# A fourth unit of seven products in the first down-projection, and sums of weights made ahead and kept in DRAM

## The chip, the cores and the metric

The kernel runs on one core of a Trainium2 chip. Its time is the device time of one execution in microseconds, and times of several executions are told as a median with the lowest and the highest. A profile of one further execution shows every instruction of the five engines: TensorE (PE, matrix products; PEld, the loading of its stationary operand), VectorE (DVE), ScalarE (ACT), GpSimd (POOL) and SyncE (SP, which issues nearly all transfers here).

## The reference, cut to what matters

Two transformer layers on 256 tokens of width 1024 in float32. Each layer has an attention and then a gated feed-forward block with a causal convolution of width 3:

```python
def conv_ffn(h, w_up, conv_w, conv_b, w_down):
    S_ = h.shape[1]
    u = h @ w_up
    up = jnp.pad(u, ((0, 0), (CONV_W - 1, 0), (0, 0)))
    u = conv_b + sum(conv_w[j] * up[:, j:j + S_] for j in range(CONV_W))
    gate, val = jnp.split(u, 2, axis=-1)
    return (jax.nn.silu(gate) * val) @ w_down

for l in range(DEPTH):
    ...
    x = x + o.transpose(0, 2, 1, 3).reshape(B_, S_, N_HEADS * HEAD_DIM) @ w_o
    x = x + conv_ffn(rmsnorm(x, ffn_norm[l]), w_up[l], conv_w[l], conv_b[l], w_down[l])
return rmsnorm(x, final_norm)
```

`w_up` is 1024 x 5632 and `w_down` 2816 x 1024 in each layer. The change concerns `w_down` and the loading of the weights.

## The kernel before

**Weights.** All weights come from DRAM in units of 128 x 2048 float32 (1 MB), numbered in the order of use: the attention of layer 0, 22 units of its up-projection (`U_UP0` on), its down-projection (`U_DN0` on), the projections of layer 1's attention, and the same two for layer 1. `fetch` loads a unit into one of three raw buffers ("raw", `wr` in the trace; loads are L184). `prepare` plans the work on it: ScalarE copies it to a rounded high part (`hi_part`, L216, `wh`), VectorE subtracts to get the low part (`lo_part`, L224, `wl`). Each has four buffers. A product is made of three matmuls on `F32R` operands: high activations by high weights, high by low, low by high. `used(i)` says that unit i's matmuls have been written down, and plans the preparation of unit i + 4. When the last low part of a unit is written down, its raw buffer is given to the unit three places on in the order of loads (`NEXT`).

**Up-projection.** Each of the 22 units gives 128 gate and 128 value columns in 48 matmuls (L780 to L782). `post` makes the convolution taps, the gate and high and low parts of the result (L817 to L837), four buffers of 256 columns, one pair of units to a tile.

**Down-projection.** `Down` walks over eleven units (i = 0 to 10); each is two blocks of 128 rows, with 256 tokens as two blocks of 128 and 1024 output columns as two halves of 512. An ordinary unit is eight block products of three matmuls with 512 columns (`mm`, L635 to L638). A unit in `SEVEN` is done in seven block products (`seventh`, L662 to L664), by a scheme that needs four sums of activation blocks (`mix` on GpSimd, `split` L852 and L856 for their high and low parts) and four sums of weight blocks. Those sums form a unit of their own, the "ninth" (`SUMS`): number `slot(layer, i) + 1`, right behind unit i's. It isn't loaded: `sums_of` makes it on VectorE from unit i's raw buffer, in one addition of 1024 columns (L199) and two of 512 (L203), into two buffers of the pool "q". Then it gets high and low parts like any unit (`wh<-sums`, `wl<-sums`). Of unit i itself only three of four column blocks get a high and a low part. Four of the seven products go to PSUM banks of their own (`one`, `six`, `five`, `sev`), three to the ordinary accumulators (`a00`, `a01`, `a10`). After the last unit of seven, `gather` adds the four banks into the residual `xr` (L676 on VectorE and GpSimd, one copy L679 on ScalarE). Layer 0 has seven products in units 3, 5 and 7, layer 1 in 3, 5, 7 and 8. Units 9 and 10 come last, row block by row block, and `add` (L754) adds each accumulator to `xr`; then PE transposes `xr` (L336) for the next projection.

**Order.** TensorE's order is written by hand. The other work is put off with `chain`: steps with due times on a clock that counts TensorE's work, which `tick` runs when they are due and `need` or `require` when a product asks for them. From the first attention on, a planner may shift instructions of the engines around that order.

At the end of layer 1, `tail` (L1206 on) handles the last 512 columns in two halves of 256; it follows a chain of squares, roots and scalings on ScalarE and VectorE.

Of the kernel before, what the change touches and what calls it, by code (L numbers as in the profile page):

```python
# [7 lines left out]
F32 = mybir.dt.float32  # L8
# [3 lines left out]
ALU = mybir.AluOpType  # L12
AX = mybir.AxisListType

P = 128
# [14 lines left out]
UNIT = 2048  # L30
# [20 lines left out]
U_UP0 = 16  # L51
U_DN0 = U_UP0 + NF

SEVEN = ((3, 5, 7), (3, 5, 7, 8))
U_KV = U_DN0 + NF // 2 + len(SEVEN[0])
U_QB = U_KV + 2
U_OB = U_QB + 4
U_UP1 = U_OB + 4
U_DN1 = U_UP1 + NF
N_UNITS = U_DN1 + NF // 2 + len(SEVEN[1])  # L60


def slot(layer, i):
    return (U_DN0, U_DN1)[layer] + i + sum(k < i for k in SEVEN[layer])


SUMS = [slot(l_, i_) + 1 for l_ in range(2) for i_ in SEVEN[l_]]
RAW = {}
for k_ in range(N_UNITS):
    if k_ not in SUMS:  # L70
        RAW[k_] = len(RAW)
NEXT = {k_: min((j_ for j_ in RAW if RAW[j_] == n_ + 3), default=N_UNITS) for k_, n_ in RAW.items()}


@with_exitstack
def trunk(ctx: ExitStack, tc, x, xw, pos, cpk, fin, w, out):
    nc = tc.nc
    one = ctx.enter_context(tc.tile_pool(name="one", bufs=1))
    qd = ctx.enter_context(tc.tile_pool(name="qd", bufs=15))
    wk = ctx.enter_context(tc.tile_pool(name="wk", bufs=2))  # L80
    wp = ctx.enter_context(tc.tile_pool(name="wp", bufs=4))
    ps = ctx.enter_context(tc.tile_pool(name="ps", bufs=2, space=bass.MemoryType.PSUM))

    uid = [0]

# [49 lines left out]
    clock = [0.0]  # L135
    put_off = []
# [8 lines left out]
    def tick(ns):  # L145
        clock[0] += ns
        while put_off and not busy[0]:
            item = min(put_off, key=lambda t: t[0])
            if item[0] > clock[0]:
                return  # L150
            run_item(item)
# [13 lines left out]
    def require(*key):  # L165

        while True:
            mine = [t for t in put_off if t[1] == key]
            if not mine:
                return  # L170
            run_item(min(mine, key=lambda t: t[0]))
# [5 lines left out]
    raws = {}  # L177
    w_time = [0.0]

    def fetch(i):  # L180
        if i < N_UNITS and i not in SUMS:
            raws[i] = wp.tile([P, UNIT], F32, tag="raw", name=f"wr{i}", bufs=3)
            for c in (slice(0, UNIT // 2), slice(UNIT // 2, UNIT)) if 2 <= i < 10 else (slice(0, UNIT),):
                nc.sync.dma_start(raws[i][:, c], w[RAW[i]][:, c])  # L184

    def raw_of(i, c):

        if i not in SUMS:
            return raws[i][:, c]
        t, at = raws[i][c.start // 1024], c.start % 1024  # L190
        return t[:, at:at + c.stop - c.start]
# [38 lines left out]
    def weights(i):  # L230
        wq[i] = (spaced(wp, UNIT, F32R, "hi", f"wh{i}", 4),
                 spaced(wp, UNIT, F32R, "lo", f"wl{i}", 4))

    def prepare(i):

        if i >= N_UNITS:
            return
        n = 4 if i <= 5 or 1 <= i - U_UP0 <= 3 or 1 <= i - U_UP1 <= 3 or U_KV <= i <= U_OB else 2
        cut = [slice(k * UNIT // n, (k + 1) * UNIT // n) for k in range(n)]
        w_time[0] = max(clock[0] + 200.0, w_time[0] + (2500.0 if i - 1 in SUMS else 4500.0), 34000.0 if i == 7 else 0.0)  # L240
        if i == U_KV + 1:
            w_time[0] = max(w_time[0], clock[0] + 3300.0)

        def first():
            if i in SUMS:
                require("t", i)
            weights(i)
            hi_part(i, cut[0])

        def last():  # L250
            lo_part(i, cut[-1])
            if i + 1 in SUMS:
                require("t", i + 1)
            if i not in SUMS:
                fetch(NEXT[i])
            if i + 2 in SUMS:
                sums_of(i + 2)

        if i + 1 in SUMS:
            cut[1] = slice(UNIT // 2, 3 * UNIT // 4)  # L260
        steps = [(w_time[0] - clock[0], first)]
        for k in range(n - 1):
            steps.append((2000.0 / n, lambda k=k: lo_part(i, cut[k])))
            steps.append((2000.0 / n, lambda k=k: hi_part(i, cut[k + 1])))
        chain(("w", i), *steps, (2000.0 / n, last))

    def used(i):

        prepare(i + 4)
# [16 lines left out]
    for c in range(KC):  # L286
        t, at = (first[c // 2], KC * (c == 1) + c % 2 * CH) if c < 6 else (first[c - 3], 0)
# [329 lines left out]
    class Down:  # L617
# [26 lines left out]
        def seventh(self, i):  # L644

            u = self.at(i)
            need(u)
            need(u + 1)
            self.wait(i)
            if not self.more:  # L650
                self.more = [bank(t) for t in ("u", "t", "u", "t")]
            one, five, six, sev = self.more
            (rh, rl), (th, tl) = wq[u], wq[u + 1]
            xh, xl = self.parts[2 * i]
            (a00, a01), (a10, _) = self.acc
            own = dict(start=i == SEVEN[self.layer][0], stop=i == SEVEN[self.layer][-1])
            for o, x_, hi, lo, k, mine in ((one, 0, rh, rl, 0, True), (six, 6, th, tl, 2, True), (five, 5, th, tl, 0, True),
                                           (sev, 4, th, tl, 1, True), (a00, 2, rh, rl, 1, False), (a01, 7, rh, rl, 2, False),
                                           (a10, 3, th, tl, 3, False)):
                o, wh, wl = pairs(o), turns(hi[:, half(k)]), turns(lo[:, half(k)])  # L660
                c = blk(x_)
                nc.tensor.matmul(o, xh[:, c], wh, start=mine and own["start"], stop=False)  # L662
                nc.tensor.matmul(o, xh[:, c], wl, start=False, stop=False)
                nc.tensor.matmul(o, xl[:, c], wh, start=False, stop=mine and own["stop"])  # L664
                tick(3 * 512 / 2.4)
            if own["stop"]:
                self.gather()

# [16 lines left out]
        def units(self, lo, hi):  # L685
            for i in range(lo, hi):
                if self.layer is not None and i in SEVEN[self.layer]:
                    self.seventh(i)
                    used(self.at(i))
                    used(self.at(i) + 1)  # L690
                    yield 21 * 512 / 2.4
                    continue
                for k in range(2):
                    for b in range(NB):
                        self.mm(i, k, b, range(2))
                        yield 6 * 512 / 2.4
                used(self.at(i))
# [52 lines left out]
        def add(self, b, n, after):  # L750
            def half_add(m):
                c = slice(m * S, (m + 1) * S)
                x_ = xr[b][:, half(n)][:, c]
                op = nc.vector.tensor_tensor(out=x_, in0=self.acc[b][n][:, c], in1=x_, op=ALU.add)  # L754
                if self.short and (b, n, m) == (1, 0, 0):
                    tc.keep_in_program_order(op)

            chain(("x", b, n), (150.0, lambda: half_add(0)), (300.0, lambda: half_add(1)),
                  (300.0, lambda: after(b, n)))
# [561 lines left out]
```

## Time and profile before

| | us |
|---|---|
| median of 3 executions | 543.51 |
| lowest, highest | 542.98, 543.75 |
| the profiled execution | 543.93 |
| its span, first to last instruction | 542.2 |

The profile's stages, by TensorE's work in the trace:

| stage | from to, us |
|---|---|
| up-projection, layer 0 | 112 to 231 |
| down-projection, layer 0 | 231 to 287 |
| keys, queries and attention, layer 1 | 287 to 362 |
| up-projection, layer 1 | 362 to 481 |
| down-projection, layer 1 | 481 to 536 |

A row of the timeline gives the start, the duration, engine, line, operation, tiles (written from read), shape and count; in brackets stands how long the engine had been idle and what ended that. The duration of a matmul is longer than its distance from the next, since they overlap: the distance of starts is what counts. A row of the windows gives for a stretch of time each engine's busy time with its number of instructions, the granted TensorE clock, the busy share of the DMA engines and their rate.

### The profile page before, as it was taken

The numbers are of one execution on the slowest core, as the hardware profiler recorded it, in microseconds if no ns is written. First come the engines' busy times: TensorE is split into PE (matmuls) and PEld (weight loads), VectorE is DVE, ScalarE is ACT, GpSimd is POOL, SyncE is SP. The second block draws the span as 40 slices with busy tenths as digits, with TensorE's granted clock in tenths as the row PEclk, the third lists the DMA queues.
The fourth block names the chain that finished last, engine by engine and source line by source line (L and its number), as shares of the span: only waits on it lengthen the run. The fifth ranks groups of instructions, "written<-read, shape, count | busy, mean of one in ns | idle before, by whom it ended". The sixth has DMA issues, their size and how long they took to land.

```text
span 542.2 us, 9977 instructions
## 1 busy us (share of the span) xinstructions
PE 533.7 (98%) x3721; PEld 490.5 (90%) x3721; DVE 459.7 (85%) x910; ACT 384.7 (71%) x740; POOL 153.6 (28%) x196
## 2 busy tenths in 40 slices
PE   9999999999999999999999999999999999999995
PEld 7888888899999999988888887789999999998884
DVE  6698868689798988889999788889889788798995
ACT  6989776679576676666568798787657767666644
POOL 7322101012424533140011165202434345231004
PEclk9999999999999999999999999999999999999999
DMA  8974544442466655644664644243375556554511
GB/s 310 399 257 166 204 156 163 150 146 88 163 231 229 233 192 202 228 156 155 233 233 176 218 151 157 79 144 97 149 254 213 183 210 242 221 195 155 165 69 77
DMA packets 16464, 100.99 MB, mean 186 GB/s; under 512 B 1952, under 2 KB 2080, under 8 KB 5920
## 3 DMA queue, kind: packets, MB, share of 16 engines
q1 hardware_dynamic: 16128, 100.09, 51.5%
q8 instruction: 29, 0.48, 0.3%
q10 hardware_dynamic: 288, 0.26, 0.1%
q14 instruction: 19, 0.16, 0.1%
HBM read 99.30 MB, written 1.05 MB: 185 GB/s over the span
## 4 chain that ended last, share of the span: by engine, by line
PE 79%; DVE 10%; ACT 6%; issue 2%; POOL 1%; DMA 1%; DVEq 0%; SPq 0%; POOLq 0%; ACTq 0%
PE u L781 7%; PE u L782 7%; PE u L780 7%; PE t L780 6%; PE t L782 6%; PE t L781 6%; PE acc L393 5%; PE acc L395 5%; PE acc L394 5%; DVE wl L224 4%; PE acc L638 4%; PE acc L635 4%; PE acc L636 4%; ACT m L516 2%; PE acc L782 2%
## 5 line engine op out<-in xcount | busy, mean ns | idle before, releaser
L224 DVE TENSOR_TENSOR wl<-wr,wh 128x1024 fp32r<-128x1024 f32 (+1 forms) x186 | 200.8, 1097 | 21.5 <-ACT wh L216 21.0
L216 ACT ACTIVATE wh<-wr 128x1024 fp32r<-128x1024 f32 (+1 forms) x190 | 174.1, 942 | 25.0 <-issue 5.8
L780 PE MATMUL u<-q,wh 128*128 128x256 f32 x320 | 88.4, 277 | 0.0
L781 PE MATMUL u<-q,wh 128*128 128x256 f32 x320 | 88.2, 276 | 0.1
L782 PE MATMUL u<-q,wl 128*128 128x256 f32 x320 | 88.0, 275 | 0.0
L828 POOL TENSOR_TENSOR m<-m,m 128x256 f32<-128x256 f32 x30 | 50.0, 1666 | 114.0 <-DVE m L823 82.2
L781 PE MATMUL t<-q,wh 128*128 128x256 f32 x288 | 79.3, 275 | 0.0
L782 PE MATMUL t<-q,wl 128*128 128x256 f32 x288 | 79.3, 275 | 0.0
L780 PE MATMUL t<-q,wh 128*128 128x256 f32 x288 | 79.3, 275 | 0.0
L635 PE MATMUL acc<-wh,q 128*128 128x512 f32 x182 | 71.0, 390 | 0.2 <-ACT q L593 0.2
L636 PE MATMUL acc<-wl,q 128*128 128x512 f32 x182 | 69.5, 382 | 0.0
L781 PEld LDWEIGHTS u<-q,wh 128*128 128x128 f32 x320 | 61.5, 192 | 0.3 <-DVE q L357 0.3
L782 PEld LDWEIGHTS u<-q,wl 128*128 128x128 f32 x320 | 61.5, 192 | 0.0
L780 PEld LDWEIGHTS u<-q,wh 128*128 128x128 f32 x320 | 61.3, 192 | 0.0
L638 PE MATMUL acc<-wh,q 128*128 128x512 f32 x182 | 58.3, 381 | 0.0
L780 PEld LDWEIGHTS t<-q,wh 128*128 128x128 f32 x288 | 55.3, 192 | 0.0
L782 PEld LDWEIGHTS t<-q,wl 128*128 128x128 f32 x288 | 55.3, 192 | 0.0
L781 PEld LDWEIGHTS t<-q,wh 128*128 128x128 f32 x288 | 55.3, 192 | 0.0
L393 PE MATMUL acc<-wh,q 128*128 128x512 f32 x128 | 50.0, 391 | 0.0
L394 PE MATMUL acc<-wl,q 128*128 128x512 f32 x128 | 48.8, 381 | 0.0
L395 PE MATMUL acc<-wh,q 128*128 128x512 f32 x128 | 48.6, 380 | 0.0
L836 ACT ACTIVATE q<-m 128x256 fp32r<-128x256 f32 x30 | 12.3, 416 | 40.8 <-POOL m L828 40.8
(215 smaller groups left out, 1193.3 us busy)
## 6 DMA issues: line engine op xcount, KB each, us to landing
wr<-in_w SPq DMA_DIRECT2D x82, 1024.0 KB, 4.8
wr<-in_w SPq DMA_DIRECT2D x16, 512.0 KB, 6.8
first<-in_xw SPq DMA_DIRECT2D x7, 384.0 KB, 6.2
xr<-in_x SPq DMA_DIRECT2D x2, 512.0 KB, 8.6
fin_t<-in_fin SPq DMA_DIRECT2D x1, 512.0 KB, 6.5
out<-ot SPq DMA_DIRECT2D x1, 512.0 KB, 2.6
first<-in_xw SPq DMA_DIRECT2D x1, 388.0 KB, 3.5
out<-m ACTq DMA_DIRECT2D x1, 256.0 KB, 2.1
```

Of the source, the lines that this page charges most:

```text
L216: nc.scalar.activation(wq[i][0][:, c], raw_of(i, c), AF.Copy, **({} if g is None else {"scale": g}))
L224: nc.vector.tensor_tensor(out=lo, in0=raw, in1=hi, op=ALU.subtract)
L393: nc.tensor.matmul(o, xh[:, blk(b)], wh, start=(c == 0), stop=False)
L394: nc.tensor.matmul(o, xh[:, blk(b)], wl, start=False, stop=False)
L395: nc.tensor.matmul(o, xl[:, blk(b)], wh, start=False, stop=(c == KC - 1))
L635: nc.tensor.matmul(o, ph[:, blk(b)], turns(hi[:, s_]), start=first, stop=False)
L636: nc.tensor.matmul(o, ph[:, blk(b)], turns(lo[:, s_]), start=False, stop=False)
L638: nc.tensor.matmul(o, pl[:, blk(b)], turns(hi[:, s_]), start=False, stop=end)
L780: nc.tensor.matmul(o, hi[:, s_], xh, start=(c == 0), stop=False)
L781: nc.tensor.matmul(o, hi[:, s_], xl, start=False, stop=False)
L782: nc.tensor.matmul(o, lo[:, s_], xh, start=False, stop=(c == KC - 1))
L828: nc.gpsimd.tensor_tensor(out=h, in0=gs, in1=t[1], op=ALU.mult)
```

## The change

Unit 8 of layer 0's down-projection becomes a unit of seven products. In both layers the ninth unit that belongs to unit 8 is made in the up-projection: before up-unit 12, a raw buffer is loaded with unit 8's four blocks in another order (three transfers), four additions of 512 columns on VectorE turn it into the sums, it is stored in DRAM, and the buffer is given on. `SEQ` is the new order of loads with these entries, and `fetch` now works through it by places. In the down-projection the stored unit is loaded like any other, through the raw buffers; of unit 8 itself only the 1536 columns that it still needs. The ninth units of 3, 5 and 7 are made as before. Due times of the preparations around a stored unit are 2300 instead of 2500 or 4500. In `seventh` the products come in another order: those with the unit's own weights first (one, a00, a01), then those with the ninth unit's (six, five, sev, a10), and `used` for the first is called after three products instead of seven.

```diff
-SEVEN = ((3, 5, 7), (3, 5, 7, 8))
+SEVEN = ((3, 5, 7, 8), (3, 5, 7, 8))
...
+AHEAD = ({8: U_UP0 + 12}, {8: U_UP1 + 12})
...
-NEXT = {k_: min((j_ for j_ in RAW if RAW[j_] == n_ + 3), default=N_UNITS) for k_, n_ in RAW.items()}
+EARLY = {at_: [slot(l_, i_) + 1] for l_ in range(2) for i_, at_ in AHEAD[l_].items()}
+STORED = [k_ for t_ in EARLY.values() for k_ in t_]
+SEQ = []
+for k_ in range(N_UNITS):
+    SEQ += [("sums", j_) for j_ in EARLY.get(k_, ())]
+    if k_ not in SUMS or k_ in STORED:
+        SEQ.append(k_)
...
+    dr = ctx.enter_context(tc.tile_pool(name="dr", bufs=1, space=bass.MemoryType.DRAM))
...
+    def fetch(p):
+        free.add(p)
+        while at_load[0] in free and at_load[0] < len(SEQ):
+            at_load[0] += 1
+            load(at_load[0] - 1)
+
+    def load(p):
+        i = SEQ[p]
+        if i not in RAW and i not in STORED:
+            ahead(p, i[1])
+            return
+        raws[i] = wp.tile([P, UNIT], F32, tag="raw", name=f"wr{i}", bufs=3)
+        if i in STORED:
+            require("ahead", i)
+            nc.sync.dma_start(raws[i], stored[i])
+            return
+        for c in (slice(0, UNIT // 2), slice(UNIT // 2, UNIT)) if 2 <= i < 10 else (slice(0, 1536 if i + 1 in STORED else UNIT),):
+            nc.sync.dma_start(raws[i][:, c], w[RAW[i]][:, c])
+
+    def ahead(p, i):
+
+        raw = wp.tile([P, UNIT], F32, tag="raw", name=f"ws{i}", bufs=3)
+        t, src = (v.rearrange("p (k n) -> p k n", k=4) for v in (raw, w[RAW[i - 1]]))
+        stored[i] = dr.tile([P, UNIT], F32, name=f"sums{i}")
+        for to, k in ((slice(0, 3, 2), slice(0, 3, 2)), (slice(1, 2), slice(3, 4)), (slice(3, 4), slice(1, 2))):
+            nc.sync.dma_start(t[:, to], src[:, k])
+
+        def add(o, a, b):
+            return lambda: tc.keep_in_program_order(
+                nc.vector.tensor_tensor(out=t[:, o], in0=t[:, a], in1=t[:, b], op=ALU.add))
+
+        def store():
+            nc.sync.dma_start(stored[i], raw)
+            fetch(p + 3)
+
+        chain(("ahead", i), (8000.0, add(0, 0, 1)), (1000.0, add(1, 1, 2)), (1000.0, add(2, 0, 2)), (1000.0, add(3, 2, 3)),
+              (700.0, store))
...
-        w_time[0] = max(clock[0] + 200.0, w_time[0] + (2500.0 if i - 1 in SUMS else 4500.0), 34000.0 if i == 7 else 0.0)
+        w_time[0] = max(clock[0] + 200.0, w_time[0] + (2300.0 if i - 1 in STORED or i in STORED else 2500.0 if i - 1 in SUMS else 4500.0), 34000.0 if i == 7 else 0.0)
...
-            if i not in SUMS:
-                fetch(NEXT[i])
-            if i + 2 in SUMS:
+            if i in SEQ:
+                fetch(SEQ.index(i) + 3)
+            if i + 2 in SUMS and i + 2 not in STORED:
                 sums_of(i + 2)
...
-            for o, x_, hi, lo, k, mine in ((one, 0, rh, rl, 0, True), (six, 6, th, tl, 2, True), (five, 5, th, tl, 0, True),
-                                           (sev, 4, th, tl, 1, True), (a00, 2, rh, rl, 1, False), (a01, 7, rh, rl, 2, False),
-                                           (a10, 3, th, tl, 3, False)):
+            for o_, (o, x_, hi, lo, k, mine) in enumerate(((one, 0, rh, rl, 0, True), (a00, 2, rh, rl, 1, False), (a01, 7, rh, rl, 2, False),
+                                           (six, 6, th, tl, 2, True), (five, 5, th, tl, 0, True), (sev, 4, th, tl, 1, True),
+                                           (a10, 3, th, tl, 3, False))):
...
+                if o_ == 2:
+                    used(u)
+            used(u + 1)
             if own["stop"]:
                 self.gather()
...
                     self.seventh(i)
-                    used(self.at(i))
-                    used(self.at(i) + 1)
```

More of the change, by code (lines that the diff above doesn't have):

```diff
@@ L178, in trunk @@
     w_time = [0.0]
[L180 to L184, printed above, removed]
+    stored = {}
+    free = set()
+    at_load = [2]
+    def fetch(p):
[29 more added lines that the diff above has]
+              (700.0, store))
     def raw_of(i, c):
-        if i not in SUMS:
+        if i not in SUMS or i in STORED:
             return raws[i][:, c]
@@ L244, in first @@
         def first():
-            if i in SUMS:
+            if i in SUMS and i not in STORED:
                 require("t", i)
+            while i not in raws:
+                require("ahead", next(t[1][1] for t in put_off if t[1][0] == "ahead"))
             weights(i)
@@ L251, in last @@
             lo_part(i, cut[-1])
-            if i + 1 in SUMS:
+            if i + 1 in SUMS and i + 1 not in STORED:
                 require("t", i + 1)
-            if i not in SUMS:
-                fetch(NEXT[i])
-            if i + 2 in SUMS:
+            if i in SEQ:
+                fetch(SEQ.index(i) + 3)
+            if i + 2 in SUMS and i + 2 not in STORED:
                 sums_of(i + 2)
```

## The prediction

> **What bounds the kernel now.** I read the head of the page first, then the waits of TensorE, then the windows by stage, then the timeline of both down-projections.
>
> ```profile
> span 542.2 us, 9977 instructions
> PE 533.7 (98%) x3721; PEld 490.5 (90%) x3721; DVE 459.7 (85%) x910; ACT 384.7 (71%) x740; POOL 153.6 (28%) x196
> ```
> ```profile
> PE u L663 <- DVE wl L224: 0.4, 1, 0.4
> ```
> ```profile
> core 0: us, PE busy (x) PEld busy (x) DVE busy (x) ACT busy (x) POOL busy (x), PEclk, DMA share, GB/s
> 140.00:231.00 91.00, 91.00 (x816) 91.00 (x816) 78.02 (x121) 62.67 (x102) 30.37 (x29) 1.00 0.61 216
> 231.00:287.00 56.00, 56.00 (x267) 48.88 (x266) 51.03 (x68) 35.43 (x51) 8.70 (x12) 1.00 0.54 188
> 478.00:529.00 51.00, 50.57 (x247) 44.37 (x246) 48.03 (x57) 30.02 (x37) 4.65 (x3) 1.00 0.42 152
> ```
> TensorE is busy in every microsecond of the up-projection (140 to 231) and of the first down-projection (231 to 287), at the full granted clock (1.00). In the second down-projection (478 to 529) 0.43 us are missing, and the one wait in this work is L663, the second matmul of a product. A busy engine isn't proof, so I look at the distance from start to start. Units 7 (of seven products) and 8 (of eight) of the first down-projection:
>
> ```profile
> 265.81 0.38 PE L662 MATMUL u<-wh,q 128*128 128x512 f32 x1
> ...
> 270.34 0.38 PE L635 MATMUL acc<-wh,q 128*128 128x512 f32 x1
> ...
> 275.52 0.38 PE L635 MATMUL acc<-wh,q 128*128 128x512 f32 x1
> ```
> Twenty-one matmuls take 4.53 us and 24 take 5.18 us: 0.216 us each both times, so they run without a gap. Here time is the number of matmuls. In the second down-projection unit 8 already has seven products, right behind unit 7, and there the rhythm breaks:
>
> ```profile
> 520.84 0.38 PE L662 MATMUL u<-wh,q 128*128 128x512 f32 x1
> 521.64 0.48 PE L663 MATMUL u<-wl,q 128*128 128x512 f32 x1 [0.43 <-DVE wl L224]
> 521.97 0.38 PE L664 MATMUL u<-wh,q 128*128 128x512 f32 x1
> ```
> The steps are 0.80 and 0.33 us instead of 0.216: 0.58 + 0.11 = 0.70 us are lost. L663 is the second product ("six"), the first one that reads the ninth unit, and it waits for that unit's low part. VectorE and ScalarE before it:
>
> ```profile
> 516.09 1.22 DVE L199 TENSOR_TENSOR sums<-wr 128x1024 f32<-128x1024 f32 x1
> 517.23 0.68 DVE L224 TENSOR_TENSOR wl<-wr,wh 128x512 fp32r<-128x512 f32 x1
> 517.83 1.41 DVE L203 TENSOR_TENSOR sums<-sums,wr 128x512 f32<-128x512 f32 x2
> 519.16 2.43 DVE L224 TENSOR_TENSOR wl<-sums,wh 128x1024 fp32r<-128x1024 f32 x2
> ```
> ```profile
> 519.28 1.06 ACT L216 ACTIVATE wh<-sums 128x1024 fp32r<-128x1024 f32 x1 [0.79 <-DVE sums L203]
> ```
> VectorE goes from the sums straight to the low parts, which end at 521.59; L663 starts 0.05 us later. From start to start an operation of 1024 columns takes 1.14 us (516.09 to 517.23), one of 512 takes 0.60 (517.23 to 517.83). So the sums, 1.14 + 2 x 0.60 = 2.34 us, are what makes the ninth unit late.
>
> **The change, part by part.**
>
> *Fewer matmuls in the first down-projection.* Unit 8 loses 3 of 24: 3 x 0.216 = **-0.65 us**, since TensorE has no gap there. By the Trainium skill ("TensorE: Matmul & The Clock Gate", Back-to-back issue gap) a stream of 512-column matmuls runs at about 131 ns each, which would make this term -0.39 us and the time 542.3, inside the forecast's own range. This trace has 216 ns in a stream with no gap, so the measurement decides.
>
> *The stall in the second one.* Two edits remove it. The ninth unit comes from DRAM as a finished unit, so 2.34 us of VectorE sums go from the queue ahead of its low parts. And the product order becomes one, a00, a01, six...: the ninth unit is first read at the fourth product, 2 x 3 x 0.216 = 1.30 us later than now. Either is more than the 0.70 us lost. What is late next? The ninth unit's load and its weight buffer, both of which unit 6 leaves behind:
>
> ```profile
> 506.22 1.22 DVE L224 TENSOR_TENSOR wl<-wr,wh 128x1024 fp32r<-128x1024 f32 x1
> ```
> ```profile
> 515.66 0.38 PE L662 MATMUL u<-wh,q 128*128 128x512 f32 x1
> ```
> ```profile
> 517.43 1.06 ACT L216 ACTIVATE wh<-sums 128x1024 fp32r<-128x1024 f32 x1 [3.88 <-DVE sums L199]
> ```
> Unit 6's last low part ends at 507.4; with the 4.8 us of a load (row below) the ninth unit lands at 512.2, ahead of its high part now at 517.43. The weight buffer is free when unit 7 starts, at 515.66; two high parts and the last low part behind them take some 4 us from there, and the fourth product starts 30 matmuls, 6.5 us, after it. Cover about 2.5 us: **-0.70 us**.
>
> *The tail.* The end is near two limits:
>
> ```profile
> 529.09 0.38 PE L638 MATMUL acc<-wh,q 128*128 128x512 f32 x1
> 529.64 0.74 DVE L754 TENSOR_TENSOR xr<-acc,xr 128x256 f32<-128x256 f32 x2
> 530.42 0.63 ACT L369 ACTIVATE m<-xr 128x512 f32<-128x512 f32 x1 [5.82 <-DVE xr L754]
> 535.71 0.28 PE L746 MATMUL u<-wh,q 128*128 128x256 f32 x1
> 536.36 0.41 DVE L1206 TENSOR_TENSOR xr<-u,xr 128x256 f32<-128x256 f32 x1
> ```
> The last matmul ends at 535.99, but its reader L1206 starts 0.37 us later, behind a ScalarE chain that began with L754, and L754 started 0.17 us after its matmuls' end (529.47) because VectorE was busy with the gather. With fewer sums that lateness can go: between 0 and -0.17 us; I take **-0.1 us**.
>
> *Sums in the up-projections.* Each layer adds three loads (1 MB), four additions, a 1 MB store and a 1 MB load back. The additions:
>
> ```profile
> L203 DVE TENSOR_TENSOR sums<-sums,wr x14: 674/686/1042, 232.3 to 518.6; 128x512 f32<-128x512 f32 x14
> ```
> 4 x 0.69 = 2.74 us of VectorE, which has 91.00 - 78.02 = 13.0 us free there. Their cover is the lead of the weights, seen on the unit that the store's buffer holds up, up-unit 14 of layer 0 (the load in the buffer that the sums will get, then unit 14's load, first high part, last low part and first matmul):
>
> ```profile
> 154.96 0.33 SPq L184 DMA_DIRECT2D wr<-in_w  x1
> ```
> ```profile
> 165.57 0.33 SPq L184 DMA_DIRECT2D wr<-in_w  x1
> ```
> ```profile
> 175.04 1.05 ACT L216 ACTIVATE wh<-wr 128x1024 fp32r<-128x1024 f32 x1
> ```
> ```profile
> 179.87 1.22 DVE L224 TENSOR_TENSOR wl<-wr,wh 128x1024 fp32r<-128x1024 f32 x1
> ```
> ```profile
> 187.96 0.28 PE L780 MATMUL u<-q,wh 128*128 128x256 f32 x1
> ```
> ```profile
> wr<-in_w SPq DMA_DIRECT2D x82, 1024.0 KB, 4.8
> ...
> out<-ot SPq DMA_DIRECT2D x1, 512.0 KB, 2.6
> ```
> The weights end at 181.09, 6.9 us early. With the change unit 9's buffer, free at 154.96, goes to the sums; by the due times in the diff (8.0 + 1.0 + 1.0 + 1.0 + 0.7) the store goes out at 166.7. No store of 1 MB is in this trace. Lower bound 2.6 us, the whole output row; twice that row, for twice the bytes, is 5.2; upper bound 10.4 us, four times that row. I take 5.2, next to the load's 4.8: landed 171.9. SP's queue holds the store until the fourth addition is done and then unit 14's load until the store has landed; behind them stands only unit 15's load, issued at 169.53 now and needed 5.4 us after unit 14. Unit 14's load lands at 171.9 + 4.8 = 176.7, so its high part starts 1.7 us later and its weights end at 182.8, 5.2 us early. **Cost 0**, each microsecond beyond 5.2 costs one. That leaves the cover at 0 for a store of 10.4 us. Where an addition waits for a late load, the low parts behind it on VectorE wait too, under the same cover.
>
> *VectorE in the first down-projection.* Unit 8 adds two low parts of the ninth unit and one split of the activations (L856, 1024 columns), and drops one 512-column low part: 3 x 1.14 - 0.60 = +2.8 us, against 5.0 us idle in the 56. In a unit of seven the buffers of its own weights are free earlier, after three products. From unit 7 on, the low parts of units 8 (ninth), 9 and 10 can follow each other as their buffers come free, ending near 274, when TensorE needs units 9 and 10 at 274.9 and 277.5: cover 1 to 3 us. Cost 0, upper bound 0.8 (first rival).
>
> *Sum*: -0.65 - 0.70 - 0.10 = -1.45 us. The profiled execution took 543.93 us (span 542.2 and 1.7 around it), which gives 542.48. The median shown, 543.51, is 0.42 lower, so on that scale **542.1 us**. Own range 541.6 to 542.5: no tail gain or all of it, and 0.3 us for an order of VectorE and ScalarE that is planned anew in the attention between the layers.
>
> **The rivals.**
>
> *The gather moves into the residual adds (gain mostly kept in the second layer).* The gather starts 4.5 us later, and nothing of unit 8 stands between it and the adds any more:
>
> ```profile
> 279.19 0.38 PE L638 MATMUL acc<-wh,q 128*128 128x512 f32 x1
> 279.64 0.74 DVE L754 TENSOR_TENSOR xr<-acc,xr 128x256 f32<-128x256 f32 x2
> 281.35 0.60 PE L336 MATMUL t<-ident,xr 128*128 128x128 f32 x4
> ```
> ```profile
> 277.65 2.07 DVE L226 SCALAR_TENSOR_TENSOR wl<-wr,cp,wh 128x512 fp32r<-128x512 f32 x3
> ```
> Now the add ends at 280.38, 0.97 us ahead of the transposes that read it. From the gather's start to its add TensorE will need 18 matmuls, 3.9 us; VectorE may have six gather operations of 0.60 and four low parts of the next projection (L226) of 0.66, 6.2 us, less some 0.6 that run early. All ahead of the add: 6.2 - 0.6 - 3.9 - 0.97 = 0.8 us of stall, 542.9 (542.5 to 543.3). For it: the transposes also need the two banks that the gather reads. Against: layer 1 has the same order today and its add was 0.17 us late. Chance 0.26.
>
> *The stall of the second layer stays*, because weight buffers and not the sums hold the low part: then only unit 8's matmuls are won, 542.9. Against: ScalarE's row names the sums. Chance 0.10.
>
> *Slower: the store holds the raw ring.* If it lands later than 10.4 us after issue, layer 0 stalls, and with the same cover layer 1 too. The gain of 1.45 is used up where 2 x (L - 10.4) = 1.45, at L = 11.1 us; at 13 us the stalls are 2 x 2.6 and the time is 543.5 - 1.45 + 5.2 = 547.3. For it: DMA engines are 0.61 busy here, the sums' loads add more. Against: 512 KB reached DRAM in 2.6 us. The Trainium skill ("DMA: Bandwidth & Descriptors", Anatomy of one DMA) calls the completion of writes to HBM surprisingly long at times; the one row here shows none. Chance 0.14.
>
> **How the numbers follow.** Forecast 0.50, rivals 0.26, 0.10 and 0.14. A measurement of this kernel tells 0.2%, 1.1 us, from no change: below 542.4 is faster. The forecast gives 0.50 faster (its edge above 542.4 is too thin to count), the first two rivals 0.36 same, the third 0.14 slower. The range 541.4 to 543.8 takes in the forecast and the first two rivals with both bounds, and leaves most of the third out.
>
> **What would show it.** Right: unit 8 of layer 0 at 4.53 us; no step over 0.3 us in unit 8 of layer 1; TensorE without waits from 140 to 231; the store landing about 5 us after issue; L754 within 0.3 us of its matmuls. Wrong: TensorE waiting for low parts in an up-projection, or at L336 near 281. A store over 10 us, or a gather that blocks the adds, would make the prediction wrong.

## The result, and the profile after

| | median, us | lowest to highest | executions |
|---|---|---|---|
| before, in the same session | 543.44 | 542.96 to 544.07 | 8 |
| after | 547.86 | 545.62 to 550.78 | 8 |

The change makes the kernel slower: ratio 1.0086, 95% interval 1.0059 to 1.0113, that is 4.4 us more, where the forecast had 1.4 us less. The executions also scatter over 5.2 us, where those of before lie within 1.1.

The page of the profiled execution of after (547.99 us), its head and the waits of TensorE:

```profile
span 546.3 us, 10010 instructions
PE 534.6 (98%) x3718; PEld 490.6 (90%) x3718; DVE 465.9 (85%) x916; ACT 387.4 (71%) x741; POOL 157.7 (29%) x200
```
```profile
PE t L385 <- DVE xr L804: 1.7, 1, 1.7
```

There are three matmuls fewer, as there should be, and TensorE's busy time has grown by 0.9 us all the same. The wait at L663 is gone; a longer one has come, at the transposes (L385, before L336) behind the residual add (L804, before L754). The windows by stage say where:

```profile
140.00:231.00 91.00, 91.00 (x818) 91.00 (x817) 78.52 (x123) 62.38 (x100) 35.24 (x34) 1.00 0.66 240
231.00:275.14 44.14, 44.14 (x208) 38.75 (x206) 40.27 (x45) 28.26 (x35) 6.04 (x10) 1.00 0.52 190
275.14:290.78 15.64, 13.88 (x62) 11.04 (x61) 14.39 (x29) 9.69 (x21) 2.65 (x2) 0.89 0.54 199
478.00:529.00 51.00, 51.00 (x265) 45.53 (x264) 46.58 (x55) 32.53 (x42) 5.30 (x3) 1.00 0.47 170
```

TensorE is full in the up-projection (91.00 of 91.00), in layer 0 up to the end of the units of seven, and in the second down-projection (51.00 of 51.00, where before had 50.57). The 15.64 us of units 9 and 10 in layer 0 are the exception: 1.76 us without work, and a granted clock of 0.89. From start to start of the stages' first matmuls, before against after (the timeline's starts that the prediction doesn't show are these, of before and of after):

```profile
287.37 0.38 PE L393 MATMUL acc<-wh,q 128*128 128x512 f32 x1
...
525.42 0.38 PE L635 MATMUL acc<-wh,q 128*128 128x512 f32 x1
```
```profile
266.07 0.38 PE L711 MATMUL u<-wh,q 128*128 128x512 f32 x1
...
275.14 0.38 PE L684 MATMUL acc<-wh,q 128*128 128x512 f32 x1
...
290.78 0.38 PE L442 MATMUL acc<-wh,q 128*128 128x512 f32 x1
...
519.11 0.38 PE L711 MATMUL u<-wh,q 128*128 128x512 f32 x1
...
528.17 0.38 PE L684 MATMUL acc<-wh,q 128*128 128x512 f32 x1
...
538.47 0.28 PE L796 MATMUL u<-wh,q 128*128 128x256 f32 x1
```

| part | before | after | difference | forecast |
|---|---|---|---|---|
| layer 0, units 7 and 8 | 9.71 | 9.07 | -0.64 | -0.65 |
| layer 0, units 9 and 10 with the transposes among them | 11.85 | 15.64 | **+3.79** | 0, at most 0.8 |
| layer 1, units 7 and 8 | 9.76 | 9.06 | -0.70 | -0.70 |
| from the last matmul's start to the end of the span | 6.47 | 7.80 | **+1.33** | -0.10 |
| all the rest | | | +0.3 | 0 |
| span | 542.2 | 546.3 | +4.1 | -1.45 |

In these two traces both gains came to within 0.01 us. Two losses in places that the forecast held to be covered are nearly four times as large.

**The stall.** VectorE at the end of layer 0's down-projection in the kernel after:

```profile
271.01 2.36 DVE L271 TENSOR_TENSOR wl<-wr,wh 128x1024 fp32r<-128x1024 f32 x2 [0.59 <-ACT wh L263]
274.17 1.23 DVE L271 TENSOR_TENSOR wl<-wr,wh 128x1024 fp32r<-128x1024 f32 x1 [0.80 <-ACT wh L263]
275.31 0.68 DVE L728 TENSOR_TENSOR xr<-u,xr 128x512 f32<-128x512 f32 x1
275.91 0.68 DVE L728 TENSOR_TENSOR m<-u,m 128x512 f32<-128x512 f32 x1
276.51 1.22 DVE L271 TENSOR_TENSOR wl<-wr,wh 128x1024 fp32r<-128x1024 f32 x1
277.64 1.28 DVE L728 TENSOR_TENSOR m<-t,m 128x512 f32<-128x512 f32 x2
278.84 0.68 DVE L728 TENSOR_TENSOR xr<-xr,m 128x512 f32<-128x512 f32 x1
279.44 0.68 DVE L728 TENSOR_TENSOR xr<-xr,t 128x512 f32<-128x512 f32 x1
280.04 1.84 DVE L273 SCALAR_TENSOR_TENSOR wl<-wr,cp,wh 128x512 fp32r<-128x512 f32 x2
281.80 0.68 DVE L728 TENSOR_TENSOR xr<-xr,m 128x512 f32<-128x512 f32 x1
282.40 0.74 DVE L804 TENSOR_TENSOR xr<-acc,xr 128x256 f32<-128x256 f32 x2
```
```profile
278.81 0.38 PE L687 MATMUL acc<-wh,q 128*128 128x512 f32 x1
...
282.87 0.83 PE L385 MATMUL t<-ident,xr 128*128 128x128 f32 x4 [1.74 <-DVE xr L804]
```

The accumulator that L804 adds is done at 278.81 + 0.38 = 279.2; L804 starts at 282.40, 3.2 us later (0.07 us in the kernel before). From 274.17 to 282.40 VectorE has no gap: its operations stand in the order in which they run, and the two low parts of unit 10 (274.17, 276.51) and the gather (L728) are ahead of L804. So are two low parts of the next projection (L273). The low parts of unit 10 are late because VectorE waited twice for ScalarE (0.59 and 0.80 us), and ScalarE for a transfer:

```profile
269.92 2.00 ACT L263 ACTIVATE wh<-wr 128x1024 fp32r<-128x1024 f32 x2 [1.59 <-DMA wr<-in_w]
273.08 1.06 ACT L263 ACTIVATE wh<-wr 128x1024 fp32r<-128x1024 f32 x1 [1.16 <-DMA wr<-in_w]
```

The second is unit 10's high part. SP's queue, unit 10's load before and after:

```profile
261.41 0.33 SPq L184 DMA_DIRECT2D wr<-in_w  x1
```
```profile
268.18 0.33 SPq L212 DMA_DIRECT2D wr<-in_w  x1
```

6.8 us later, while unit 7 of TensorE's work starts only 0.26 us later. There are three raw buffers, handed round in the order of loads. Before, unit 10 took the buffer of unit 7; now the stored ninth unit stands in the ring too, unit 9 takes that buffer (its load goes out at 264.17), and unit 10 must wait until the last low part of unit 8 itself is written (268.15). The load then lands at 272.97, in the middle of unit 8's seven products, which end at 275.14; in the kernel before it landed at 266.14, before unit 8 began.

So the ring accounts for 4.0 of the 6.8 us (268.18 against 264.17). The other 2.8 are there without it, since unit 7's own last low part is late (263.45, before 260.69). VectorE is 1.5 us behind already at the start of this down-projection (its first sums at 232.52 instead of 231.03), and the fourth unit's split (L906) now stands ahead of unit 7's low parts:

```profile
261.19 1.22 DVE L906 TENSOR_TENSOR q<-q,q 128x1024 fp32r<-128x1024 f32 x1
262.32 1.82 DVE L271 TENSOR_TENSOR wl<-wr,wh 128x1024 fp32r<-128x1024 f32 x2
```

**The clock.** Right behind the stall (three windows; PE busy, granted clock, DMA share, rate):

```profile
282.00:284.30 2.30, 1.43 (x8) 1.00 0.00 0
284.40:287.70 3.30, 3.28 (x10) 0.50 0.37 114
287.80:290.78 2.98, 2.98 (x18) 1.00 0.49 206
```

For 3.3 us TensorE's granted clock is 0.50, which costs 1.65 us. With the 1.76 us without work that is 3.4 of the 3.79 us; the other 0.4 lie in single steps above 0.216 us beside the transposes.

**The tail.** In layer 1 the same queue is late without making TensorE wait: ScalarE waited 2.32 us for unit 10's load at 525.58, and the residual add came at

```profile
532.66 1.05 DVE L728 TENSOR_TENSOR xr<-xr,m 128x512 f32<-128x512 f32 x1
533.63 0.74 DVE L804 TENSOR_TENSOR xr<-acc,xr 128x256 f32<-128x256 f32 x2
```

though the accumulator was done at 531.84 + 0.38 = 532.2. From L804 runs the chain of squares and roots that ends the kernel. Its head is 1.4 us behind the accumulator (0.17 before), and the end of the span is 1.33 us further from the last matmul than before.

### The profile page after: what moved, and what is told of

It reads as the page before. It is cut to its first block, busy times and chain, and to the rows that moved or that the text cites. A ratio compares the mean times of both kernels' runs of the same rounds, so it can differ in the third digit from the quotient of the medians.

```text
span 546.3 us, 10010 instructions
## 1 busy us (share of the span) xinstructions
PE 534.6 (98%) x3718; PEld 490.6 (90%) x3718; DVE 465.9 (85%) x916; ACT 387.4 (71%) x741; POOL 157.7 (29%) x200
## 4 chain that ended last, share of the span: by engine, by line
PE 73%; DVE 13%; ACT 7%; DMA 3%; issue 3%; POOL 1%; SPq 0%; DVEq 0%; ACTq 0%
PE u L831 7%; PE u L832 7%; PE u L830 6%; DVE wl L271 6%; PE t L831 6%; PE t L830 6%; PE t L832 6%; PE acc L442 5%; PE acc L444 5%; PE acc L443 5%; PE acc L687 3%; PE acc L685 3%; PE acc L684 3%; ACT m L565 2%; DMA wr<-in_w 2%
## 5 line engine op out<-in xcount | busy, mean ns | idle before, releaser
L271 DVE TENSOR_TENSOR wl<-wr,wh 128x1024 fp32r<-128x1024 f32 (+1 forms) x190 | 203.0, 1090 | 23.3 <-ACT wh L263 23.1
L263 ACT ACTIVATE wh<-wr 128x1024 fp32r<-128x1024 f32 (+1 forms) x194 | 177.3, 942 | 32.2 <-DMA wr<-in_w 10.9
L878 POOL TENSOR_TENSOR m<-m,m 128x256 f32<-128x256 f32 x28 | 44.5, 1591 | 108.0 <-DVE m L873 38.8
L684 PE MATMUL acc<-wh,q 128*128 128x512 f32 x174 | 68.5, 394 | 0.2 <-ACT q L642 0.2
L685 PE MATMUL acc<-wl,q 128*128 128x512 f32 x174 | 67.0, 385 | 0.0
L687 PE MATMUL acc<-wh,q 128*128 128x512 f32 x174 | 56.4, 384 | 0.0
L442 PE MATMUL acc<-wh,q 128*128 128x512 f32 x128 | 50.0, 391 | 0.0
L443 PE MATMUL acc<-wl,q 128*128 128x512 f32 x128 | 48.8, 382 | 0.0
L444 PE MATMUL acc<-wh,q 128*128 128x512 f32 x128 | 48.7, 380 | 0.0
```

The lines of the kernel that those rows point to most:

```text
L263: nc.scalar.activation(wq[i][0][:, c], raw_of(i, c), AF.Copy, **({} if g is None else {"scale": g}))
L271: nc.vector.tensor_tensor(out=lo, in0=raw, in1=hi, op=ALU.subtract)
L442: nc.tensor.matmul(o, xh[:, blk(b)], wh, start=(c == 0), stop=False)
L443: nc.tensor.matmul(o, xh[:, blk(b)], wl, start=False, stop=False)
L444: nc.tensor.matmul(o, xl[:, blk(b)], wh, start=False, stop=(c == KC - 1))
L684: nc.tensor.matmul(o, ph[:, blk(b)], turns(hi[:, s_]), start=first, stop=False)
```

## The experiments

Three theories, each of which speaks to a different part of the change. **A**: the new order of products puts the gather and the add behind low parts. **B**: VectorE has too much to do (the fourth unit's split and low parts). **C**: the stored unit in the ring of raw buffers makes the loads of units 9 and 10 late. Times are medians; each ratio is to executions of the kernel before on the same chip.

### Parts of the change alone

Four kernels ran beside each other (before: 543.25). The order of products of before, everywhere, in the kernel after:

```diff
-((one, 0, rh, rl, 0, True), (a00, ...), (a01, ...), (six, ...), (five, ...), (sev, ...), (a10, ...))
+((one, 0, rh, rl, 0, True), (six, ...), (five, ...), (sev, ...), (a00, ...), (a01, ...), (a10, ...))
...
-                if o_ == 2:
+                if o_ == 5:
```

> The changed kernel with the products in the order of before (one, six, five, sev, a00, a01, a10); the unit's own weights are then free after the sixth product. Theory A (the new order of products hands the gather its banks 1.3 us later): the stall before the transposes of layer 0 shrinks from 1.9 us to under 0.8 and the half clock behind it (3.4 us of records at 0.5) goes, the tail of layer 1 loses some 1.3 us: 542.5 to 544. Theory B (VectorE has too much to do in front of the residual adds, the order of products is beside the point): stall and half clock stay, 546 to 549.

Measured 544.35 (543.25 to 545.2), ratio 1.0020 [1.0009, 1.0031]. No wait at the transposes and full clock; 3.3 of the 4.4 us are gone. The one new wait is in the rotary part of the next projection: `PE t L483 <- DVE m L477`, 0.71 us. That is for A, or for any theory in which VectorE's queue is only a little too late. It isn't a cure of the loads: those of units 9 and 10 go out at 263.71 and 267.68, only 0.5 us earlier than in the changed kernel. What differs is the order on VectorE:

```profile
280.81 1.40 DVE L804 TENSOR_TENSOR xr<-acc,xr 128x256 f32<-128x256 f32 x4
...
283.13 0.68 DVE L728 TENSOR_TENSOR xr<-xr,m 128x512 f32<-128x512 f32 x1
```

One operation of the gather and one low part of the next projection now stand behind the add. Counted from unit 9's first matmul the add starts after 5.39 us, against 7.26 in the changed kernel and 4.12 before. So late loads alone don't make the stall; they do together with what stands ahead of the add.

Stored sums in layer 1 alone, with the new order and with the old one:

```diff
-SEVEN = ((3, 5, 7, 8), (3, 5, 7, 8))
+SEVEN = ((3, 5, 7), (3, 5, 7, 8))
...
-AHEAD = ({8: U_UP0 + 12}, {8: U_UP1 + 12})
+AHEAD = ({}, {8: U_UP1 + 12})
```

> The changed kernel with layer 0 as before (three units of seven, nothing stored for it), layer 1 with the stored sums and the new product order. Both theories: the 3.8 us lost at the end of layer 0 go and 0.65 us of matmuls come back, so some 3.1 us less than the changed kernel, 544 to 545.3; layer 1 alone then shows -0.7 for its stall and +1.2 for its tail against before. If the time is at 543 or less, the tail is not a matter of layer 1's own edits.

> As the kernel with layer 0 as before, but with the products in the order of before too. Theory A: the residual adds of layer 1 come on time, the tail is short, the stall of unit 8 stays away since the sums come from DRAM: 542.5 to 543.1. Theory B: the tail stays 1.2 us longer, as with the new order: 544 to 545.

Measured 545.16 (543.52 to 546.05), ratio 1.0032 [1.0022, 1.0041], and 544.15 (543.17 to 545.16), ratio 1.0013 [1.0003, 1.0023]. Layer 1's half of the change, whose traces have at most 0.17 of the 0.70 us of stall left, is a loss by itself, by 1.9 us or 0.9. So not all of the loss is the first layer's fourth unit, and B alone can't be it: in layer 1 no product was added. The trace of the first (543.52, the fastest of ten) hardly shows its loss. That of the second has the short tail that A asked for, and a wait of 0.57 us inside the units of seven (L712), so its time is in B's range for a reason that B doesn't name.

The fourth unit of seven alone, in the kernel before, with its sums made in place:

```diff
-SEVEN = ((3, 5, 7), (3, 5, 7, 8))
+SEVEN = ((3, 5, 7, 8), (3, 5, 7, 8))
```

> The kernel before with one edit, unit 8 of layer 0 as a fourth unit of seven, its sums made on VectorE where they are used; old product order, nothing stored. Theory A: the banks of the gather are ready early, so a stall of about 0.7 us in unit 8 as in layer 1 before, and little at the transposes: 543.4 to 544.2. Theory B: VectorE has 2.3 us more to do than in the changed kernel, so the stall before the transposes is as long or longer, with half clock: 546 to 550.

Measured 544.34 (543.98 to 544.59), ratio 1.0018 [1.0009, 1.0027]: the extra work on VectorE costs more than three matmuls bring. Its trace has two new waits in layer 0, of 0.29 us (L663) and 0.23 (L336), and units 9 and 10 take 12.54 us instead of 11.85. Layer 1's code is that of the kernel before, and yet its units 7 and 8 run without the stall:

```profile
516.67 0.38 PE L662 MATMUL u<-wh,q 128*128 128x512 f32 x1
...
525.74 0.38 PE L635 MATMUL acc<-wh,q 128*128 128x512 f32 x1
```

They take 9.07 us, not 9.76: TensorE gets there 1.0 us later than in the trace of before, and the sums are ready. So that stall depends on which of the two engines is ahead, and one trace of the kernel before doesn't tell how often it occurs.

The executions of this kernel lie within 0.6 us. Among these four the wide scatter belongs to the kernels in which a stored sum goes through the raw ring (a later trial shows that the ring isn't needed for it).

### One remedy for each theory

Four more beside each other (before: 543.39). For A, the old order only in the unit after which the gather comes; for C, the stored sums loaded into two buffers of the pool "q" and not into the ring; for B, the split of the activations (L906) moved to GpSimd; and the three together.

```diff
+            if own["stop"]:
+                order = [order[k_] for k_ in (0, 3, 4, 5, 1, 2, 6)]
...
-                if o_ == 2:
+                if o_ == (5 if own["stop"] else 2):
```

> The changed kernel with the products of before in the last unit of seven of each layer alone (the one whose banks the gather reads). Theory A (gather late by the new order): as with the old order everywhere, or a little better since the other units keep the later reading of their sums: 543.0 to 544.4, and its traces show no half clock inside the span. Theory B (VectorE's load and late loads of weights): no better than the old order everywhere, 544.4 or more.

```diff
-    if k_ not in SUMS or k_ in STORED:
+    if k_ not in SUMS:
         SEQ.append(k_)
...
+    def load_sums(i):
+        require("ahead", i)
+        raws[i] = [quad(F32, "sums").rearrange("p c t -> p (c t)") for _ in range(2)]
+        for h in range(2):
+            nc.sync.dma_start(raws[i][h], stored[i][:, h * 1024:(h + 1) * 1024])
...
+            if i + 3 in STORED:
+                load_sums(i + 3)
```

> The changed kernel, but the stored sums are loaded into two buffers of the pool q, as the sums of the other units, so the ring of three raw buffers carries one unit less in each down-projection; new product order. Theory C (the extra unit makes the loads of units 9 and 10 late, VectorE stands and the gather queues behind their low parts): ScalarE no longer waits for loads near 273 and 525, the stall before the transposes is under 1 us: 543.5 to 545.5. Theory A alone: the stall and the half clock stay, 547 to 549.

```diff
-                  (800.0, lambda: nc.vector.tensor_tensor(out=lo, in0=raw, in1=f(hi), op=ALU.subtract)))
+                  (800.0, lambda: nc.gpsimd.tensor_tensor(out=lo, in0=raw, in1=f(hi), op=ALU.subtract)))
```

> The changed kernel with the low part of the split activations (four operations of 1024 columns a layer, 1.14 us each) on GpSimd. Theory B (VectorE's amount of work): 4.6 us less of it ahead of the gather, so raw buffers come free earlier too; stall under 1 us: 543.5 to 545.5. Theories A and C: at most a part of it, 546 to 548.

> The three edits together: old products in the last unit of seven, stored sums in q buffers, split's low part on GpSimd. If A, B and C are all there is, TensorE runs without a gap through both down-projections, the tail is as before: before less 0.65 and 0.70, 541.9 to 542.6. If it stays at 543.2 or above, something else of the change costs what it wins, in the up-projections for instance.

| remedy | median | ratio, interval |
|---|---|---|
| A: old order in the last unit of seven | 547.32 | 1.0078 [1.0060, 1.0095] |
| C: stored sums outside the ring | **543.66** | 1.0002 [0.9993, 1.0011] |
| B: split on GpSimd | 551.97 | 1.0150 [1.0129, 1.0171] |
| all three | 548.85 | 1.0099 [1.0077, 1.0120] |

Of these four only C's remedy works: it takes back 4.2 us, and no difference from the kernel before is left. Its trace shows the same chain: unit 10's load, its high part, the residual add and two waits of TensorE.

```profile
264.50 0.33 SPq L208 DMA_DIRECT2D wr<-in_w  x1
```
```profile
270.71 1.06 ACT L265 ACTIVATE wh<-wr 128x1024 fp32r<-128x1024 f32 x1 [0.70 <-DMA wr<-in_w]
```
```profile
280.57 0.68 DVE L732 TENSOR_TENSOR xr<-xr,m 128x512 f32<-128x512 f32 x1
281.17 0.74 DVE L808 TENSOR_TENSOR xr<-acc,xr 128x256 f32<-128x256 f32 x2
```
```profile
281.64 0.83 PE L389 MATMUL t<-ident,xr 128*128 128x128 f32 x4 [1.03 <-DVE xr L808]
...
284.29 0.44 PE L389 MATMUL t<-ident,xr 128*128 128x128 f32 x2 [0.52 <-DVE q L399]
```

The load goes out 3.7 us earlier (264.50 against 268.18) and the high part starts 2.4 us earlier. The add gains less: TensorE itself is 0.53 us earlier in this trace, and from unit 9's first matmul (274.61) the add starts after 6.56 us instead of 7.26. The two waits are 1.55 us together instead of 1.74, so the expected "under 1 us" was missed, and ScalarE still waits 0.70 us for unit 10's load. Units 9 and 10 take 13.85 us, 2.00 more than before; of the 1.79 us won there 1.65 are the half clock, which this trace doesn't have. The tail is 542.5 - 536.15 = 6.3 us, 1.4 shorter. So in the traces the remedy's gain is the clock and the tail, and the stall of layer 0 has another cause beside the ring.

Theory A in that form falls (the order in the last unit alone leaves waits of 1.53 and 0.52 us, at full clock). Why the old order everywhere brought so much more isn't settled. B's remedy makes things worse, but that doesn't refute B: on GpSimd the split takes 2.9 us instead of 1.2, so the low part comes later than before. The same edit is in the kernel with all three, whose trace has waits of 0.50 us in a unit of seven of each layer. The groups of the profile, on GpSimd and on VectorE:

```profile
L906 POOL TENSOR_TENSOR q<-q,q 128x1024 fp32r<-128x1024 f32 x8 | 23.3, 2908 | 15.3 <-ACT q L902 12.5 <-DVE wl L271 2.7
```
```profile
L906 DVE TENSOR_TENSOR q<-q,q 128x1024 fp32r<-128x1024 f32 x8 | 9.7, 1217 | 0.0
```

### What is left of the wait, and a version that beats both

Three kernels with C's remedy (before: 543.27): with the old order everywhere as well; with the preparation of the first key/value unit put off, so that its low parts stand behind the gather and L804 on VectorE; and with layer 1's half alone.

```diff
-            if i == U_KV + 1:
+            if i in (U_KV, U_KV + 1):
                 tc.keep_in_program_order(op)
...
+        if i == U_KV:
+            w_time[0] = max(w_time[0], clock[0] + 6500.0)
```

> The changed kernel with the stored sums in two query buffers, and the preparation of the first key/value unit put off, so that the gather, the add of the eleventh unit and the residual add stand ahead of that unit's low parts in VectorE's order. If what is left (1.2 + 0.68 us of TensorE at the transposes after the first down-projection) comes from the low parts that stand ahead of the residual add: the stall falls to about 0.5 us, and the time to 541.9 to 542.8. If it comes from the late high parts of units 9 and 10 alone: no change from 543.66 (543.3 to 544.0). If the key/value unit is then late itself, TensorE waits for its low part after the transposes, and the time is 543.7 to 545.

Measured **542.62** (541.99 to 543.82), ratio 0.9987 [0.9978, 0.9996]: faster than both kernels, by 0.65 us against before, and as expected for low parts that stand ahead of the add. Order and windows at that place:

```profile
278.41 1.06 DVE L734 TENSOR_TENSOR xr<-xr,m 128x512 f32<-128x512 f32 x1
279.39 0.74 DVE L810 TENSOR_TENSOR xr<-acc,xr 128x256 f32<-128x256 f32 x2
280.06 0.74 DVE L275 SCALAR_TENSOR_TENSOR wl<-wr,cp,wh 128x512 fp32r<-128x512 f32 x1
```
```profile
231.00:275.14 44.14, 44.14 (x208) 38.67 (x206) 41.28 (x47) 29.57 (x36) 6.04 (x10) 1.00 0.55 199
275.14:290.40 15.26, 15.26 (x79) 13.14 (x78) 15.04 (x31) 11.49 (x27) 2.65 (x2) 1.00 0.40 144
```

The add starts at 279.39, 4.25 us behind unit 9's first matmul (6.56 with C's remedy alone, 4.12 before), no key/value part (L275) is ahead of it, and TensorE is busy in all of 15.26 us. So of the 3.14 us by which the add of the changed kernel was late, the traces give 0.70 to the ring and 2.31 to this order (one trace each, and the last one has its loads 1 us earlier too). The span is 541.0, 1.2 us less than in the trace of before. The medians differ by 0.65 us only, which is what the three matmuls alone are worth. Whether putting the key/value unit off would also do without C's remedy was not tried.

> The changed kernel with two edits at once: the stored sums are loaded into two buffers of the query weights instead of the ring of three raw buffers, and the products of a unit of seven stand in the order of the kernel before, everywhere. Theory C (the ring makes the loads of units 9 and 10 late): with the loads out of the ring there is no late high part for the order of products to be behind, so the old order brings little over the ring's cure alone (543.66): 543.2 to 543.8. Theory A (the order of products puts the gather and the residual add behind low parts): the old order takes away what is left of the stall of 1.2 + 0.68 us at the transposes, and the time falls to 541.8 to 542.5. A stall of 0.3 to 0.9 us inside the units of seven, as the trials with the old order showed, would be the old order's own price.

> The stored sums in two query buffers, in layer 1 alone; layer 0 keeps the three units of seven of the kernel before, but with the new order of products. Theory C: the stall of the ninth unit in layer 1 goes (0.7 us), the tail stays at about 6.4 us, and nothing is added in layer 0: 542.6 to 542.9. If the order of products costs by itself in layer 0: 543.3 to 544.

The old order with C's remedy took 545.62 (543.18 to 547.69), ratio 1.0033 [1.0017, 1.0049], outside both ranges: A and C don't add up. Layer 1's half with C's remedy took 543.55 (542.84 to 544.70), ratio 1.0003 [0.9995, 1.0012]. Theory C's range was missed; the time lies in the range that was set for a price of the new order itself. There is no loss any more, and none of the 0.7 us that its trace no longer has as a stall can be measured. To see what the slower executions of the first of them lose, it was traced a second time, and the new order of products was put alone into the kernel before (nothing stored, three units of seven in layer 0).

> The same kernel as in the trial with the sums in query buffers and the old order of products, for a trace of one of its slower executions (they reached from 543.18 to 547.69, and the trace shown was of one near the lower end, without a stall in the units of seven). If the clock makes the scatter: a TensorE stall of 0.5 to 1 us in the first down-projection or in the key/value units, and some 3 us behind it in which matmul steps take 0.43 us instead of 0.216; time 544.5 or more. If it is not the clock: several stalls that add up to the excess over 543.2, all steps between them at 0.216 us.

> The kernel before with nothing but the new order of the seven products and the earlier release of the units' buffers: three units of seven in layer 0, no sum stored or loaded. If the order of products costs by itself, through the gather that it puts behind low parts: 543.8 to 544.8 and a stall at the transposes after the first down-projection. If it only costs where the loads of units 9 and 10 come late (theory C): 542.9 to 543.5, as the kernel before, and little scatter.

The second trace, at 545.00 us (before: 543.33), has a mean clock of 0.999, no half clock, but this, in a unit of seven of layer 0:

```profile
256.86 1.22 DVE L273 TENSOR_TENSOR wl<-sums,wh 128x1024 fp32r<-128x1024 f32 x1
```
```profile
258.13 0.48 PE L716 MATMUL u<-wl,q 128*128 128x512 f32 x1 [1.00 <-DVE wl L273]
```

In the first trace of the same kernel that low part started at 255.46, and TensorE didn't wait. VectorE had no gap between 251.7 and 261 in the second trace: it was 1.4 us behind, and so were the loads in front of it (down-unit 4 issued at 227.84 against 226.28). With the old order the ninth unit is read by the second product of seven, and such a lag falls on TensorE at once; with the new one it is the fourth, 1.3 us later. Why these loads lag isn't settled, but the sums made in the up-projection have a part in it. In the six kernels that store nothing for layer 0 the load of down-unit 4 goes out 20.4 to 21.1 us before TensorE starts unit 3; in the nine other traces, the changed kernel's (19.35) among them, it is 18.5 to 20.2 us. The new order alone took 543.41 (543.07 to 544.78), ratio 1.0005 [0.9996, 1.0014]: it costs nothing where the loads of units 9 and 10 come in time, with the gather of layer 0 still one unit earlier. Its units 7 and 8 of layer 1 take 516.09 to 525.15 = 9.06 us, without any stored sum. That stall is gone from the trace, and the time is still that of the kernel before.

## Why the prediction was wrong

- **Fewer matmuls, -0.65**: right, -0.64.
- **The stall of layer 1, -0.70**: right for the two traces, -0.70, and the rival in which the stall stays is out. As a term of the time it isn't shown. Two kernels whose traces lack the stall take as long as before (543.41 against 543.33, 543.55 against 543.27), and a trace with layer 1's code unchanged lacks it too. The forecast read it off one execution that took 0.42 us more than the median.
- **Sums in the up-projections, cost 0**: right for TensorE, which has 91.00 of 91.00 us there, and the page after has the store at 5.5 us, where 5.2 was taken:

```profile
sums<-ws SPq DMA_DIRECT2D x2, 1024.0 KB, 5.5
```

  But the store went out at 174.29, not at 166.7 as the due times said, and its raw buffer came free some 8 us later than forecast. The only slower rival, a store of over 10.4 us, did not happen. What the sums cost is time in hand: against TensorE's work the first loads of the down-projection go out 0.2 to 2.6 us later than in the kernels without them.
- **VectorE in the first down-projection, "cost 0, upper bound 0.8"**: here it failed. The step said that the low parts of units 8, 9 and 10 "can follow each other as their buffers come free, ending near 274". It counted weight buffers and left out the raw ring, which it had followed for up-unit 14 and for layer 1's ninth unit, but not for units 9 and 10. They ended at 277.73, with unit 10's load 6.8 us later than before, and units 9 and 10 took 3.79 us more. Taking the stored sums out of the ring gave back 4.2 us of the 4.4 in the medians. The step also asked only when TensorE needs those low parts. TensorE never waited for them; it waited for the add that stands behind them on VectorE. And 274 was too early in any case: with the ring cured they end at 276.5, as in the kernel before.
- **The first rival** (the gather moves into the residual adds, 0.8 us, 542.9) named the place, the line and the order on VectorE, and the edit that puts the key/value unit off bears it out: with it, on top of C's remedy, the stall is gone. Its price was too low. From the gather's start (275.31) to the add (282.40) stood seven operations of the gather where it counted six, two key/value low parts where it counted four, and a low part of unit 10 that it left out: 7.1 us instead of 5.6. TensorE was idle for 1.76, and 1.65 us of half clock came on top, which no row of the trace before could have shown.
- **The tail, -0.1**: wrong in sign in the kernel after, +1.33, with the same late load in layer 1. With the sums outside the ring it was right in the trace: 6.3 us against 6.47.

## What to carry to other kernels

When a transfer is added to a ring of buffers, follow every later user of that ring one place on, not only the added one: the loss came at the two units behind it, where no edit had been made. A lateness moves along an engine whose instructions stand in order, so the add was late in part for a load that it doesn't use, and for more by work of the next stage that stood ahead of it: look at both the first late link (the load) and the last (the order on VectorE). Count from a fixed point of TensorE's work when two traces are compared, and add up all waits of a place, or a cure looks larger than it is. And a gain that the profile shows exactly may still be lost to a queue that had 1 us of cover: write that cover down beside the gain, for each engine and each ring.

## What the runs showed of the hardware

A gap of 1.74 us in TensorE's work was followed by 3.3 us at a granted clock of 0.50 in the traced execution of after. The Trainium skill ("TensorE: Matmul & The Clock Gate", Part 1: The HAM clock gate) puts the window that decides at about 3.4 us, free-running; the length of the slow stretch agrees, while the gap before it was half as long as the idle window that the page asks for. It is no rule that such a gap costs the clock: with the split on GpSimd a gap of 2.44 us had 1.00 behind it (284.1 to 290), and with the old order in the last unit of seven one of 1.53 us had too (282 to 288). The mean clock of the eight executions of after went from 0.996 in the fastest (545.62 us) to 0.993 in the slowest (550.78), so some of their scatter is this: by an estimate from these means, 0.003 of 548 us, 1.6 of the 5.2 us.
